# The second feed-forward product of a hybrid layer as seven block products, with weight sums made by transfers

## The chip, the cores and the metric

The kernel runs on one core of a Trainium2 chip. The metric is the device time of one execution in microseconds (us), the median of the runs shown. The engines are named as in the profile: PE (TensorE, matrix products; PEld is its loading of weights), DVE (VectorE), ACT (ScalarE), POOL (GpSimd) and SP (SyncE, which here only issues transfers). A transfer (DMA) is begun by an engine's queue and carried out by sixteen transfer engines that the whole core has. Every engine works through its own instructions in a fixed order; an instruction that waits for a semaphore holds up all that stand behind it on that engine.

## What is computed

One layer of a diffusion backbone over 512 tokens of 1024 channels: a modulated norm, two token mixers (a state-space scan and a windowed attention), their merge, a residual, a second modulated norm, a gated feed-forward network with a convolution of three taps, a residual and a last norm. The part that is changed is the last product and what follows it:

```python
def conv_ffn(h, w_up, conv_w, conv_b, w_down):
    u = dwconv_centred(h @ w_up, conv_w, conv_b)
    a, b = u[..., :D_FF], u[..., D_FF:]
    return (jax.nn.silu(a) * b) @ w_down
...
        h_lat = modulate(x, norm1_g[l], sh1, sc1)
        h_ctx = modulate(ctx, norm1_g[l], csh1, csc1)
        o_lat, o_ctx = token_mixer(h_lat, h_ctx, ...)
        x = x + gt1 * o_lat
        x = x + gt2 * conv_ffn(modulate(x, norm2_g[l], sh2, sc2), ...)
...
    return rmsnorm(x, final_g)
```

`D_FF` is 2816, so `w_down` is 2816 x 1024: 22 blocks of 128 along the summed axis, 8 blocks of 128 output channels. All data are 32-bit floats.

## The kernel before

Activations lie with channels on the 128 partitions and tokens along the free axis, so a product takes a 128 x 128 block of weights and streams 512 tokens through it. To keep the accuracy of 32-bit floats, both operands are split into a high part (a rounded copy, type fp32r) and a low part (the rest), and each product of blocks is three matrix instructions: high by high, high by low, low by high (`gemm`, L190 to L201; `half_gemm`, L1730, for 256 tokens). Weights come in pieces of up to 1024 columns. `load` (L157) issues the transfer of a piece on SP's queue into one of three raw buffers, casts the high part on ACT (L152) and subtracts on DVE for the low part (L153); high and low parts have two buffers each, so a piece can only be split when PE has read the piece before the last. `run` (L170) walks a list of steps and loads one piece ahead of the step that uses it.

The first stage (L369 to L728) is recorded through a planner, `Plan` (L282): each piece of work has an engine, a cost, needs and a rank, and the planner's order is written out on PE, ACT and DVE and kept. POOL and SP are not held to that order by the planner; their instructions stand where the program's recording layer puts them. In this stage the modulation weights (16 pieces), the tokens, the context and eight blocks of mixer weights are loaded, and the first norm is worked out: sums of squares, their mean (DVE, L570), the root on POOL (L574, once for 512 tokens and once for 256 context tokens), its spread over the partitions by PE (L256) and a copy of that on ACT (L275). With the copy, DVE scales (L526), ACT casts (L528) and DVE subtracts (L530) to make the operands `hlh`, `hll` of the tokens and `hch`, `hcl` of the context. Products of the first five of eight channel blocks run on tokens that are not yet normed and are scaled afterwards (L689); the last three need the normed ones.

Then follow attention, the state-space scan and the merge (not changed). The up stage has 22 steps (`up_step`, L1857), each with two products of 8 blocks, one for the half `a` and one for the half `b` of the feed-forward network, the convolution, the gate, and the split of the result: `up_second` (L1841) multiplies on DVE (L1847), casts on ACT (L1848) and subtracts on DVE (L1849) into `F["h"]` and `F["l"]`, 22 blocks of 512 tokens each. The down stage is seven `down_step`s (L1894) and `down_last` (L1905). A `down_step` loads one of 8 blocks of output channels in three pieces of 8, 8 and 6 blocks, sums 22 x 3 products of 512 tokens in one bank of PSUM, adds it, times the gate, to the residual `x1` (L1900) and adds its square to `q3`, for the last norm. `down_last` does the eighth block in two halves of 256 tokens, so that the norm of the first half runs beside the product of the second; behind the last product come the last add, squares, sums, the root on POOL, the spread, the scaling (L1925) and the stores.

Of the kernel before, what the change touches and what calls it, by code (L numbers as in the profile page):

```python
# [9 lines left out]
F32 = mybir.dt.float32  # L10
F32R = mybir.dt.float32r
# [28 lines left out]
def raw(ap):  # L40
    return ap.bitcast(F32)
# [3 lines left out]
def tile_hybrid_layer(  # L45
# [92 lines left out]
    for i in range(2 * NFF):  # L138
        src["up", i] = wup[i], 1024

    M_LOADS = {}

    def load_raw(key):
        a, n = src[key]
        r = wpool.tile([P, 1024], F32, tag="raw", name="wraw", bufs=3)
# [236 lines left out]
    with tc.tile_pool(name="spool", bufs=1) as sp:  # L382
# [1441 lines left out]
    def close_c1():  # L1824
        c1pool.close()
        c2pool = ctx.enter_context(tc.tile_pool(name="c2pool", bufs=1, reuse_waits="tile"))
        F["h"] = c2pool.tile([P, NFF, L], F32R, name="fh")
        F["l"] = c2pool.tile([P, NFF, L], F32R, name="fl")

# [11 lines left out]
    def up_second(a, pb, t):  # L1841
        b = tmp("tc")
        i = NFF + t
        S.activation(b, pb, AF.Identity, scale=col(V_FW, 44 + i), bias=col(V_FB, i))
        V.scalar_tensor_tensor(b[:, 1:], pb[:, :-1], col(V_FW, i), b[:, 1:], ALU.mult, ALU.add)
        V.scalar_tensor_tensor(b[:, :-1], pb[:, 1:], col(V_FW, 88 + i), b[:, :-1], ALU.mult, ALU.add)
        V.tensor_tensor(a, a, b, ALU.mult)  # L1847
        S.copy(F["h"][:, t, :], a)  # L1848
        V.tensor_tensor(F["l"][:, t, :], a, raw(F["h"][:, t, :]), ALU.subtract)  # L1849

    def far_piece():

        return tuple(F[n][:, NFF - 2 : NFF, :].rearrange("p a b -> p (a b)") for n in ("h", "l"))

    ELSEWHERE["up", 1] = far_piece

# [34 lines left out]

    q3 = hpool.tile([P, L], F32, tag="q2", name="q3")

    def down_step(o):  # L1894
        def fn(*w):
            ps = accb()
            for i, n in ((0, 8), (1, 8), (2, 6)):
                gemm([(ps, F["h"], F["l"])], w[i], nk=n, k0=8 * i, first=i == 0, last=i == 2)
            xo = x1[o // 4][:, o % 4, :]
            V.scalar_tensor_tensor(xo, ps, mod2[:, 24 + o : 25 + o], xo, ALU.mult, ALU.add)  # L1900
            add_square(q3, xo, o)

        return [("dn", 3 * o + i) for i in range(3)], fn

    def down_last(*w):  # L1905

        pf = misb()
        for u in range(2):
            half_sums(pf, q3, u)
        scaled, r = {}, {}  # L1910

        def finish(u):

            z = HALF[u]
            r3 = rms_spread(r["s"], 2)
            if u:
                r3s = tmp("tc")[:, :HL]
                S.copy(r3s, rms_spread(r["s"], 2)[:, :HL])
            for i, cs in enumerate(((0,), (1,), (4,), (2, 3), (5,), (6,), (7,)) if u else ((0, 1), (2, 3), (4, 5), (6, 7))):
                for c in cs:  # L1920
                    x = x1[c // 4][:, c % 4, z]
                    if u and c in scaled:
                        G.tensor_tensor(x, scaled[c], r3s, ALU.mult)
                    else:
                        V.scalar_tensor_tensor(x, x, col(V_FG, c), r3[:, :HL], ALU.mult, ALU.mult)  # L1925
                n, c = len(cs), cs[0]
                tc.keep_in_program_order((S if c in ((1, 2, 6) if u else (2,)) else nc.sync).dma_start(
                    out[c * P : (c + n) * P, z].rearrange("(a p) t -> p a t", a=n), x1[c // 4][:, c % 4 : c % 4 + n, z]
                ))
                yield  # L1930

        def root():
            r["s"] = half_root(pf, r["sq"], 0)

        def spread():
            r["f"] = finish(0)
            next(r["f"])
            next(r["f"])

        def add(u):  # L1940
            xo = x1[1][:, 3, HALF[u]]
            if u == 0:
                V.scalar_tensor_tensor(xo, ps[u][:, :HL], mod2[:, 31:32], xo, ALU.mult, ALU.add)
                r["sq"] = half_squares([xo])
            else:

                sq = tmp("tc")[:, :HL]
                for b in range(2):
                    z = slice(b * P, (b + 1) * P)
                    V.scalar_tensor_tensor(xo[:, z], ps[u][:, z], mod2[:, 31:32], xo[:, z], ALU.mult, ALU.add)  # L1950
                    S.activation(sq[:, z], xo[:, z], AF.Square)
                r["sq"] = [sq]

        for i, c in enumerate((4, 5)):
            scaled[c] = tmp("te")[:, :HL]
            S.activation(scaled[c], x1[1][:, c % 4, HALF[1]], AF.Copy, scale=col(V_FG, c))
        ps = [accb(), accb()]
        with tc.manual_schedule(engines={mybir.EngineType.PE}):
            for u, i in ((0, 0), (1, 0), (0, 1), (0, 2), (1, 1), (1, 2)):
                half_gemm(ps[u], F["h"], F["l"], HALF[u], w[i], (8, 8, 6)[i], 8 * i, NFF, {11: root, 17: spread} if u else {})  # L1960
                if i == 2:
                    add(u)
            next(r["f"])
            r["s"] = half_root(pf, r["sq"], 1)
            for f in (r["f"], finish(1)):
                for _ in f:
                    pass
# [27 lines left out]
def pack(  # L1995
# [45 lines left out]
    d["wdn"] = _cols(w_down, A(1024))  # L2041
# [25 lines left out]
```

## Time and profile before

| | us |
|---|---|
| median of 3 runs | 1240.38 (1240.37 to 1240.45) |
| span of the profiled execution | 1239.5 |
| PE busy | 1230.0 |
| DVE busy | 864.6 |
| ACT busy | 656.3 |
| POOL busy | 145.4 |
| first stage, to the first product behind it | about 65 |
| up stage, then down stage | to 1107.7, to 1230.0 (last product) |

The profile shows one execution, taken by the hardware profiler. Its times are microseconds from the start of the span unless marked ns. A row of the timeline gives start, duration, engine, line, operation, tiles (result before the arrow, operands behind it), shape and count, and in brackets the idle time before it and what ended it. In a group row, "x154 | 60.0, 390 | 0.0" is the count, busy time in us, mean ns of one and idle time before. Products on PE are pipelined: their durations overlap, so the distance from one start to the next is what one costs. A window row gives each engine's busy time in that stretch with the number of instructions, PE's granted clock (1.00 is full speed), the mean busy share of the sixteen transfer engines and what they moved. In the row of 40 slices a digit is the busy share of a slice in tenths.

### The profile page before, as it was taken

To read this page: it belongs to the slowest core of one execution; us is meant where nothing else is said; L and a number is where in the kernel's file an instruction comes from. 1 tells how busy PE (TensorE), PEld (TensorE's weight loads), DVE (VectorE), ACT (ScalarE), POOL (GpSimd) and SP (SyncE) were. 2 spreads that over 40 slices of the span, in tenths; PEclk is the share of its full clock that TensorE was granted. 3 is DMA by queue.
4 is the path that set the end of the run, shared out by engine and by line. 5 is a ranking of instruction groups with operands and counts; after the bars stand their busy time and mean duration, and the time that the engine had idled before them with its cause. 6 is when DMAs were issued, how large, how long until landed. Compare 5 with 4: busy or idle time off the path is not lost.

```text
span 1239.5 us, 17395 instructions
## 1 busy us (share of the span) xinstructions
PE 1230.0 (99%) x6464; PEld 1013.8 (82%) x6464; DVE 864.6 (70%) x1387; ACT 656.3 (53%) x1224; POOL 145.4 (12%) x145
## 2 busy tenths in 40 slices
PE   9999999999999999999999999999999999999997
PEld 6798888888888878777787788889888888888886
DVE  5857788888645697896987767576777767772333
ACT  5658788787454476475675653224544444442221
POOL 0000000000000052261542530000100000000000
PEclk9999999999999999999999999999999999999999
DMA  9643142222354336355365577674233333333331
GB/s 371 248 136 94 56 137 81 91 72 77 119 173 132 127 102 184 115 157 158 102 187 203 146 257 262 213 231 159 89 117 119 109 113 119 112 106 97 103 94 68
DMA packets 91189, 174.57 MB, mean 141 GB/s; under 512 B 7904, under 2 KB 43552, under 8 KB 91104
## 3 DMA queue, kind: packets, MB, share of 16 engines
q1 hardware_dynamic: 90128, 172.66, 43.9%
q8 instruction: 51, 0.84, 0.3%
q10 hardware_dynamic: 976, 0.79, 0.2%
q14 instruction: 34, 0.28, 0.1%
HBM read 150.82 MB, written 17.11 MB: 135 GB/s over the span
## 4 chain that ended last, share of the span: by engine, by line
PE 93%; DMA 3%; DVE 3%; ACT 1%; issue 0%; POOL 0%; DVEq 0%; SPq 0%; ACTq 0%; POOLq 0%
PE acc L196 21%; PE acc L199 21%; PE acc L197 21%; PE score L914 3%; PE po L963 3%; PE pt L950 2%; PE mis L536 2%; PE mis L1567 2%; PE mis L1460 2%; PE mis L1575 1%; DMA wraw<-wout 1%; PE acc L1033 1%; PE acc L1034 1%; PE acc L1035 1%; PE mis L1477 1%; PE mis L1375 1%
## 5 line engine op out<-in xcount | busy, mean ns | idle before, releaser
L153 DVE TENSOR_TENSOR wlo<-wraw,whi 128x1024 fp32r<-128x1024 f32 (+2 forms) x127 | 156.0, 1228 | 125.9 <-ACT whi L152 123.0
L152 ACT CAST whi<-wraw 128x1024 fp32r<-128x1024 f32 (+2 forms) x127 | 131.2, 1034 | 196.3 <-PE acc L197 142.5
L196 PE MATMUL acc<-hlh,whi 128*128 128x512 f32 x472 | 194.2, 411 | 0.0
L197 PE MATMUL acc<-hll,whi 128*128 128x512 f32 x472 | 185.0, 392 | 0.0
L199 PE MATMUL acc<-hlh,wlo 128*128 128x512 f32 x472 | 185.0, 392 | 0.0
L196 PE MATMUL acc<-mh,whi 128*128 128x512 f32 x368 | 143.4, 390 | 0.0
L197 PE MATMUL acc<-ml,whi 128*128 128x512 f32 x368 | 143.2, 389 | 0.0
L199 PE MATMUL acc<-mh,wlo 128*128 128x512 f32 x368 | 143.2, 389 | 0.0
L199 PEld LDWEIGHTS acc<-hlh,wlo 128*128 128x128 f32 x472 | 88.6, 188 | 19.5
L196 PEld LDWEIGHTS acc<-hlh,whi 128*128 128x128 f32 x472 | 88.8, 188 | 17.9 <-issue 3.1
L197 PEld LDWEIGHTS acc<-hll,whi 128*128 128x128 f32 x472 | 88.9, 188 | 17.4 <-issue 2.4
L1462 POOL TENSOR_TENSOR st<-st,eT 128x512 f32<-128x512 f32 x24 | 29.5, 1230 | 448.7 <-ACT st L1479 435.0
L197 PEld LDWEIGHTS acc<-ml,whi 128*128 128x128 f32 x368 | 69.1, 188 | 14.4
L196 PEld LDWEIGHTS acc<-mh,whi 128*128 128x128 f32 x368 | 69.1, 188 | 14.3
L199 PEld LDWEIGHTS acc<-mh,wlo 128*128 128x128 f32 x368 | 69.1, 188 | 14.2
L1348 DVE SCALAR_TENSOR_TENSOR ta<-acc,half,ta 128x511 f32<-128x511 f32 (+1 forms) x66 | 43.9, 665 | 27.3 <-ACT ta L1347 27.1
L923 DVE CUSTOM_DVE_ANT_0 p<-score,winm,nsink 128x512 f32<-128x512 f32 (+1 forms) x64 | 51.8, 810 | 15.3 <-PE score L914 13.8
L250 POOL TENSOR_TENSOR rs<-ms,phalf 128x2 f32<-128x2 f32 (+1 forms) x5 | 4.8, 956 | 475.2 <-DVE ms L249 475.2
L196 PE MATMUL acc<-fh,whi 128*128 128x512 f32 x154 | 60.0, 390 | 0.0
L197 PE MATMUL acc<-fl,whi 128*128 128x512 f32 x154 | 59.9, 389 | 0.0
L199 PE MATMUL acc<-fh,wlo 128*128 128x512 f32 x154 | 59.9, 389 | 0.0
L1347 ACT ACTIVATE ta<-acc,half 128x512 f32<-128x512 f32 (+1 forms) x66 | 46.9, 711 | 22.5 <-PE acc L199 21.2
(381 smaller groups left out, 2891.4 us busy)
## 6 DMA issues: line engine op xcount, KB each, us to landing
wraw<-wup SPq DMA_DIRECT2D x44, 512.0 KB, 3.4
fb<-cs_d SPq DMA_DIRECT2D x32, 512.0 KB, 6.2
wraw<-wm SPq DMA_DIRECT2D x32, 512.0 KB, 3.6
wraw<-wx SPq DMA_DIRECT2D x24, 512.0 KB, 3.6
wm<-wm SPq DMA_DIRECT2D x16, 512.0 KB, 8.4
wraw<-wz SPq DMA_DIRECT2D x16, 512.0 KB, 3.5
wraw<-wos SPq DMA_DIRECT2D x16, 512.0 KB, 4.8
wraw<-wdn SPq DMA_DIRECT2D x16, 512.0 KB, 3.5
```

The source lines that it names most:

```text
L152: S.copy(hi[:, :n], r[:, :n])
L153: V.tensor_tensor(lo[:, :n], r[:, :n], raw(hi[:, :n]), ALU.subtract)
L196: T.matmul(ps, wh, xh[:, k0 + k, :], start=a, stop=False)
L197: T.matmul(ps, wh, xl[:, k0 + k, :], start=False, stop=False)
L199: T.matmul(ps, wl, xh[:, k0 + k, :], start=False, stop=b)
L536: T.matmul(ps, w[a], h[b], start=c == 1, stop=c % n == 0, skip_group_check=True)
L914: T.matmul(ps[:, o : o + len(z) * P], Q[h][:, b * P : (b + 1) * P], k[:, j, z[0] * P : (z[-1] + 1) * P], start=v == 0 and o % 512 in (0, P ...
L923: V.tensor_tensor_reduce(p[:, :w], d["ps"][i][:, o0 : o0 + w], m, op0=ALU.add, op1=ALU.min, scale=1.0, scalar=nsink[:, h : h + 1], accum_o ...
L963: T.matmul(d["po"], vst[:, cols[x], j, :], d[y][x], start=x == 0 and y == "pth", stop=x == c - 1 and y == "ptl")
L1347: S.activation(o[:, :n], ps[:, :n], AF.Identity, scale=hcol(base_w, stride + i), bias=hcol(base_b, i))
L1348: V.scalar_tensor_tensor(o[:, 1:n], ps[:, 0 : n - 1], hcol(base_w, i), o[:, 1:n], ALU.mult, ALU.add)
L1462: G.tensor_tensor(h8(n), h8(s), bc64(eT[:, z0 : z0 + 8, c]), ALU.mult)
```

## The change

The 22 blocks of the summed axis are taken as two sets of 11 (even and odd, `DK` = 11), the 8 output blocks as two halves of 4, and the tokens as two halves of 256. A product of 2 x 2 by 2 x 2 blocks is then made with seven block products instead of eight, by sums and differences of operands before the products and of results after them. Each of the seven products `j` has 4 output blocks `q`, and each of these 11 x 3 instructions of 256 tokens.

Weights: four of the seven products take sums of weight blocks. `weight_sums` makes them in DRAM, four tensors of 4 x 704 KB, by transfers on POOL's queue: a copy, and then a transfer that adds to what lies there, in pieces of 1408 bytes. It is called behind the first stage; there are 32 such transfers. The weights of a block `q` are loaded in two pieces, of 6 and 5 blocks (`DPARTS`); from the third block on the second piece of each goes to a raw buffer of its own with five places (`dnraw`, in the room of `hlh`).

Activations: in the up stage, `f_sums` splits the first half of an even block (operand of product 0), subtracts the second half and splits that (operand of product 1), and forms with the odd block the other operands. The operands of products 2 to 6 are split in the steps of the product before them (`f_split` in `down_step`), into two buffers in turn.

Results: products 0, 2 and 4 add into two banks of PSUM and are read after each; the others have a bank each. `x_add` adds them to the residual. In `down_last`, product 6, the halves change places: the second half of the tokens is finished first.

```diff
@@ in tile_hybrid_layer, the sources of the weights
-        for u, n in ((0, 8), (1, 8), (2, 6)):
-            src["dn", 3 * i + u] = wdn[i, :, u * 1024 : u * 1024 + n * P], n * P
+    DK = NFF // 2
+    DPARTS = ((0, 6), (6, DK - 6))
+    DSUMS = {i: dpool.tile([4, P, DK * P], F32, name="dsum%d" % i) for i in (1, 2, 4, 5)}
+    for q in range(4):
+        for j, t in enumerate((wdn[0, q], DSUMS[1][q], DSUMS[2][q], wdn[1, q], DSUMS[4][q], DSUMS[5][q], wdn[3, q])):
+            for u, (k0, n) in enumerate(DPARTS):
+                src["dn", (4 * j + q) * 2 + u] = t[:, k0 * P : (k0 + n) * P], n * P
+
+    def weight_sums():
+        for j, first, more in (
+            (4, wdn[0], wdn[2]), (1, wdn[2], wdn[3]), (2, DSUMS[4], wdn[3]), (5, DSUMS[2], wdn[1]),
+        ):
+            for q in range(4):
+                G.dma_start(DSUMS[j][q], first[q])
+            for q in range(4):
+                G.dma_start(DSUMS[j][q], more[q], accum_op=ALU.add, max_dma_last_dim=DK * P)
@@ behind the first stage
         run_plan(first_.order({"PE": 5.2, "ACT": 3.0, "DVE": 3.6, "SP": 0.7}, bus=2.76))
         first.update(w=ws[1], q=B_[0, "g"], k=B_[1, "g"])
+    weight_sums()
@@ the up stage
+    def f_split(s, ks, x):
+        S.copy(F["s"][s][:, 0, ks, :], x)
+        V.tensor_tensor(F["s"][s][:, 1, ks, :], x, raw(F["s"][s][:, 0, ks, :]), ALU.subtract)
+
+    def f_sums(t):
+        p, (x, y) = t // 2, F["x"]
+        e, f, g, h = (a[:, p, z] for a in (x, y) for z in HALF)
+        one = slice(p, p + 1)
+        if t % 2 == 0:
+            f_split(0, one, x[:, one, HALF[0]])
+            V.tensor_tensor(e, e, f, ALU.subtract)
+            f_split(1, one, x[:, one, HALF[0]])
+        else:
+            V.scalar_tensor_tensor(e, e, -1.0, h, ALU.mult, ALU.subtract)
+            V.tensor_tensor(f, h, f, ALU.subtract)
+            V.scalar_tensor_tensor(F["t"][:, p, :], e, -1.0, g, ALU.mult, ALU.subtract)
-        V.tensor_tensor(a, a, b, ALU.mult)
-        S.copy(F["h"][:, t, :], a)
-        V.tensor_tensor(F["l"][:, t, :], a, raw(F["h"][:, t, :]), ALU.subtract)
+        V.tensor_tensor(F["x"][t % 2][:, t // 2, :], a, b, ALU.mult)
+        f_sums(t)
@@ the down stage
+    def product(j, q, w, ps, st, after={}):
+        s = F["s"][(0, 1, 0, 1, 0, 1, 0)[j]]
+        with tc.manual_schedule(engines={mybir.EngineType.PE}):
+            for u, (k0, n) in enumerate(DPARTS):
+                wh, wl = w[u]
+                for k in range(n):
+                    c, h, l = slice(k * P, (k + 1) * P), s[:, 0, k0 + k, :], s[:, 1, k0 + k, :]
...
+                    T.matmul(ps, wh[:, c], h, start=st and k0 + k == 0, stop=False, skip_group_check=True)
+                    T.matmul(ps, wh[:, c], l, start=False, stop=False, skip_group_check=True)
+                    T.matmul(ps, wl[:, c], h, start=False, stop=en, skip_group_check=True)
-    def down_step(o):
-        def fn(*w):
-            ps = accb()
-            for i, n in ((0, 8), (1, 8), (2, 6)):
-                gemm([(ps, F["h"], F["l"])], w[i], nk=n, k0=8 * i, first=i == 0, last=i == 2)
-            xo = x1[o // 4][:, o % 4, :]
-            V.scalar_tensor_tensor(xo, ps, mod2[:, 24 + o : 25 + o], xo, ALU.mult, ALU.add)
-            add_square(q3, xo, o)
+    def down_step(j, q):
+        def fn(*w):
...
+            chain = j in (0, 2, 4)
+            bank = F["A"][q // 2] if chain else accb()
+            ps = bank[:, q % 2 * HL : q % 2 * HL + HL] if chain else bank[:, :HL]
+            product(j, q, w, ps, j == 0 and q % 2 == 0 or not chain)
+            if 1 <= j < 6:
+                ks = slice(3 * q, min(3 * q + 3, DK))
+                f_split((j + 1) % 2, ks, OPERAND[j + 1]()[:, ks, :])
+            if chain and q % 2:
+                t = tmp("te")
+                S.copy(t, bank)
...
+            elif j == 1:
+                x_add(q, 1, 1, ps)
+                x_add(4 + q, 1, -1, ps)
...
-        + [down_step(o) for o in range(7)]
-        + [([("dn", 21 + i) for i in range(3)], down_last)],
+        + [down_step(j, q) for j in range(6) for q in range(4)]
+        + [([("dn", 48 + i) for i in range(8)], down_last)],
```

More of the change, by code (lines that the diff above doesn't have):

```diff
@@ L144, in load_raw @@
         a, n = src[key]
-        r = wpool.tile([P, 1024], F32, tag="raw", name="wraw", bufs=3)
+        if key[0] == "dn" and key[1] >= 4 and key[1] % 2:
+            if "dnraw" not in F:
+                F["dnraw"] = hpool.tile([P, 5, 6 * P], F32, tag="hlh", name="dnraw")
+            r = F["dnraw"][:, key[1] // 2 % 5, :]
+        else:
+            r = wpool.tile([P, 1024], F32, tag="raw", name="wraw", bufs=3)
         dma = nc.sync.dma_start(r[:, :n], a)
@@ L1892, in tile_hybrid_layer @@
     q3 = hpool.tile([P, L], F32, tag="q2", name="q3")
[L1894 to L1909 removed]
+    ng2 = cpool.tile([P, 4], F32, name="ng2")
@@ new lines, in tile_hybrid_layer, with x_add, half_square @@
+    OPERAND = [
+        None, None, lambda: F["x"][0][:, :, HALF[0]], lambda: F["x"][1][:, :, HALF[0]], lambda: F["x"][0][:, :, HALF[1]],
+        lambda: F["x"][1][:, :, HALF[1]], lambda: F["t"],
+    ]
+    def x_add(c, u, a, ps):
+        x = x1[c // 4][:, c % 4, HALF[u]]
+        g = ng2[:, c - 4 : c - 3] if a < 0 else mod2[:, 24 + c : 25 + c]
+        V.scalar_tensor_tensor(x, ps, g, x, ALU.mult, ALU.add)
+    def half_square(c, u):
+        x, q = x1[c // 4][:, c % 4, HALF[u]], q3[:, HALF[u]]
+        if c % 4 == 0 and (c, u) in ((0, 0), (4, 1)):
+            S.activation(q, x, AF.Square)
+        else:
+            sq = tmp("tc")[:, :HL]
+            S.activation(sq, x, AF.Square)
+            V.tensor_tensor(q, q, sq, ALU.add)
@@ L1910, in down_last @@
+    def down_last(*ws):
+        ws = [ws[2 * q : 2 * q + 2] for q in range(4)]
         scaled, r = {}, {}
@@ L1930, in finish, with sums @@
                 yield
+        pf = misb()
+        def sums(u, part, first, last):
+            rms_sums(pf[:, 2 * u : 2 * u + 2], part, 2, 0, first, last)
         def root():
-            r["s"] = half_root(pf, r["sq"], 0)
+            sums(1, q3[:, HALF[1]], True, True)
+            r["s"] = rms_root(pf[:, 2:4], 2, EPS)
         def spread():
-            r["f"] = finish(0)
+            r["f"] = finish(1)
             next(r["f"])
             next(r["f"])
[L1940 to L1957, printed above, removed]
-        with tc.manual_schedule(engines={mybir.EngineType.PE}):
[L1959 to L1967, printed above, removed]
+        def early():
+            sums(0, q3[:, HALF[0]], False, False)
+            for _ in r["f"]:
+                pass
```

60 lines of the change are left out of this document (52 added, 8 removed).

## The prediction

> **What bounds the kernel now.** I read the page first (busy shares, the 40 slices), then the windows of the first 50 us, then the timelines of POOL, DVE and ACT there, last the groups and the timeline of the stage that is rewritten.
>
> ```profile
> span 1239.5 us, 17395 instructions
> PE 1230.0 (99%) x6464; PEld 1013.8 (82%) x6464; DVE 864.6 (70%) x1387; ACT 656.3 (53%) x1224; POOL 145.4 (12%) x145
> ...
> DMA  9643142222354336355365577674233333333331
> ```
>
> TensorE (PE) is busy 99% of the span, so the time is PE's work plus whatever makes PE wait. An instruction saved on PE is worth its interval; a wait added anywhere in PE's order is paid in full. The transfer engines are less than half busy in nearly all slices, except the first (31 us each).
>
> ```profile
> core 0: us, PE busy (x) PEld busy (x) DVE busy (x) ACT busy (x) POOL busy (x), PEclk, DMA share, GB/s
> 0.00:10.00 10.00, 8.85 (x60) 7.10 (x64) 2.23 (x12) 3.37 (x6) 0.78 (x9) 1.00 0.80 283
> 10.00:20.00 10.00, 10.00 (x78) 6.62 (x78) 6.40 (x15) 5.49 (x10) 0.00 (x0) 1.00 1.04 410
> 20.00:30.00 10.00, 10.00 (x79) 6.85 (x78) 6.84 (x14) 6.44 (x13) 0.00 (x0) 1.00 1.03 414
> 30.00:40.00 10.00, 10.00 (x78) 6.76 (x76) 6.16 (x16) 5.08 (x13) 1.01 (x1) 1.00 1.03 410
> 40.00:50.00 10.00, 10.00 (x66) 7.85 (x63) 9.56 (x19) 6.58 (x13) 0.70 (x1) 1.00 0.55 195
> ```
>
> From 10 to 40 us the sixteen transfer engines are full (share 1.03) at about 412 GB/s: the start-up is limited by its loads, 15.2 MB in the first 40 us, some 16 MB in the burst, 39 us of full-rate transfer. POOL does almost nothing then, but that little is on PE's path:
>
> ```profile
> 1.21 0.10 POOL L396 MEMSET rmsc<- 128x1 f32 x1
> 35.31 1.01 POOL L574 TENSOR_TENSOR rs<-ms,phalf 128x4 f32<-128x4 f32 x1 [34.00 <-DVE ms L570]
> 43.02 0.70 POOL L574 TENSOR_TENSOR rs<-ms,phalf 128x2 f32<-128x2 f32 x1 [6.70 <-DVE ms L570]
> 425.76 1.07 POOL L1462 TENSOR_TENSOR st<-st,eT 128x512 f32<-128x512 f32 x1 [382.04 <-ACT st L1479]
> ```
>
> These are the two roots of the first norm (tokens at 35.31, context at 43.02), each begun as soon as its mean is there. After them POOL is free until 425.76. What hangs on the second:
>
> ```profile
> 42.79 0.15 DVE L570 TENSOR_SCALAR ms<-acc 128x2 f32<-128x2 f32 x1
> ...
> 44.98 0.38 PE L256 MATMUL acc<-ident,rs 128*128 128x128 f32 x2
> ...
> 45.39 0.37 ACT L275 COPY r_c<-acc 128x256 f32<-128x256 f32 x1 [3.17 <-PE acc L256]
> 45.66 1.34 ACT L528 ACTIVATE hlh<-xsb,s 128x512 fp32r<-128x512 f32 x2
> ```
>
> PE and ACT run this stage in a fixed order. PE's spread at 44.98 and ACT's copy at 45.39 take the context root; behind the copy stand the casts of token operands (45.66) that PE multiplies next. A late context root therefore stops all three engines, although context itself is first multiplied some 20 us later.
>
> **The change, part by part.**
>
> *The adding transfers (the large term).* In the built order of the changed kernel POOL's queue reads: memsets; 4 copies DRAM to DRAM; 4 adding transfers, each waiting for its copy; 4 copies; 4 adding ones; 1 copy; the token root; 3 copies; 1 adding transfer, which waits for the first adding transfer of the second group and the first copy of the third; and only then the context root. Nothing holds back the first four, so they start at 1.2 us, into the full engines. Nine copies and eight adding transfers (the rest of the second group stands ahead of the third group's copy in the same queue) must be through before the context root, each of 128 x 11 x 128 floats = 704 KB.
>
> No transfer of POOL and no adding one is in this trace. The nearest prices:
>
> ```profile
> wraw<-wup SPq DMA_DIRECT2D x44, 512.0 KB, 3.4
> fb<-cs_d SPq DMA_DIRECT2D x32, 512.0 KB, 6.2
> ...
> q<-tc SPq DMA_DIRECT2D x16, 128.0 KB, 2.3
> ```
>
> A copy at the full rate: 0.721 MB / 412 GB/s = 1.75 us. An adding transfer at least the same; at most at the rate of the smallest pieces here, fb in 512-byte pieces, 704/512 x 6.2 = 8.5 us. I take twice the copy, 3.5 us, since it reads two operands, nearer to the lower row because its pieces (1408 bytes) are larger than fb's. Ahead of the context root: 9 x 1.75 + 8 x 3.5 = 44 us (30 us by the low price, 84 by the high). Full engines share these with 39 us of loads, of which the order needs nearly all by then; whoever goes first, the sum is the same: 1.2 + 39 + 44 + 2 us for a completion (the small q row) = 86 us. The mean waited from 42.94; so the root, and PE with it, is 43 us late. By the low price 1.2 + 39 + 30 + 2 = 72, 29 us late; by the high one 126, 83 us late. The token root stands behind 9 copies and 4 adding transfers, needs most of the loads as well, and comes earlier: within this term, not beside it.
>
> The Trainium skill, "DMA: Bandwidth & Descriptors", section "Issuing engines are not separate DMA queues", says transfers begun by different engines end on the same 16 transfer engines and interleave. This trace, with one busy queue, does not show it. By that rule the term is the 43 us; if POOL's queue had capacity of its own, it would be the chain alone, 1.2 + 44 + 2 = 47 us, 4 us late.
>
> *The rest of these transfers* (7 copies, 8 adding ones: 7 x 1.75 + 8 x 3.5 = 40 us) runs on into the attention part, where the engines were half full (0.55 in the last window above). Loads there are issued well ahead, but the small rearrangements (q<-tc, 2.3 us) are not, and they would share the engines: I take 3 us, from 0 to 10. They end near 150 us, far ahead of POOL's next work at 425.76 and of the use of the sums at 1107.
>
> *The up stage.* Per pair of its 22 steps the two 512-wide high/low pairs go; in come 2 casts (ACT) and 6 operations (DVE), 256 wide. On DVE:
>
> ```profile
> L1849 DVE TENSOR_TENSOR fl<-ta,fh 128x512 fp32r<-128x512 f32 x18 | 12.5, 693 | 12.4 <-ACT fh L1848 12.4
> ...
> L1925 DVE SCALAR_TENSOR_TENSOR x<-x,vec,mis 128x256 f32<-128x256 f32 x14 | 5.8, 474 | 2.9 <-PE mis L256 2.9
> ...
> 930.00:1000.00 70.00, 70.00 (x312) 57.95 (x312) 49.31 (x64) 30.43 (x39) 0.00 (x0) 1.00 0.35 113
> 1106.00:1212.00 106.00, 106.00 (x471) 87.77 (x470) 35.48 (x39) 26.61 (x32) 0.00 (x0) 1.00 0.32 95
> ```
>
> 3 x 0.47 for 0.69, 0.7 us more per 10.9 us step, with DVE at 49 of 70 us: hidden under PE's 48 products, cost 0; without that cover it would be 22 x 0.7 = 16 us, of which I allow 3.
>
> *The products.* Now 462 of 512 tokens, then 132 of 256:
>
> ```profile
> 1107.69 0.49 PE L196 MATMUL acc<-fh,whi 128*128 128x512 f32 x1
> ...
> 1212.32 0.39 PE L199 MATMUL acc<-fh,wlo 128*128 128x512 f32 x1
> ...
> 1212.55 0.28 PE L1736 MATMUL acc<-fh,whi 128*128 128x256 f32 x1
> ...
> 1215.30 0.28 PE L1738 MATMUL acc<-fh,wlo 128*128 128x256 f32 x1
> ...
> 1229.98 0.28 PE L1738 MATMUL acc<-fh,wlo 128*128 128x256 f32 x1
> ```
>
> Intervals: (1212.32 - 1107.69) / 461 = 0.227 us; (1215.30 - 1212.55) / 23 = 0.120 us, more than half of 0.227. Before: 462 x 0.227 + 132 x 0.120 = 120.7. After: 7 x 4 x 33 = 924 x 0.120 = 110.9. Seven for eight would be 15 us; at half width 9.8 us are left.
>
> *What feeds them.* The weights' high/low split grows from 176 to 308 blocks in less time, and pieces are 6 and 5 blocks (2.16 and 1.80 us of PE) in two buffers each.
>
> ```profile
> L153 DVE TENSOR_TENSOR wlo<-wraw,whi 128x768 fp32r<-128x768 f32 x8 | 7.7, 958 | 26.9 <-ACT whi L152 26.9
> L152 ACT CAST whi<-wraw 128x768 fp32r<-128x768 f32 x8 | 6.7, 837 | 28.2 <-PE acc L197 16.0 <-issue 6.9 <-PE acc L1737 5.3
> ...
> L1943 DVE SCALAR_TENSOR_TENSOR x<-acc,mod,x 128x256 f32<-128x256 f32 x1 | 0.5, 484 | 3.3 <-PE acc L1738 3.3
> ...
> 32.74 0.82 DVE L512 TENSOR_TENSOR w0l<-w,w0h 128x640 fp32r<-128x640 f32 x1 [1.07 <-ACT w0h L502]
> 39.00 0.73 ACT L502 CAST w0h<-w 128x640 fp32r<-128x640 f32 x1 [0.57 <-PE mis L536]
> ```
>
> A 6-block piece: cast 0.84 and subtraction 0.96, with some 0.3 us to the cast behind PE's last reader (a 256-wide product is out 0.28 us after its start) and an estimated 0.2 back to PE: 2.3 us, against 1.80 + 0.24 + 0.12 = 2.16 until its low part is read. So there is no slack even with both engines idle: up to 0.1 us per step. DVE's sum per product of 15.84 us: 4 x (0.96 + 0.82) + operand subtractions 3 x 0.96 + 0.69 + eight adds x 0.48 = 14.6 us; in the fifth product, with squares, about 16. And the built order puts two or three 768-wide operand subtractions between two weight subtractions just after the start of five products: some 1 us each, over 2 in the sixth. Sum of stalls: 28 x 0.05 + 6 = 7 us (from 0 to 14). The stage: -9.8 + 7 = -3 (from -10 to +4). Its loads grow to 28 x 704 KB, 178 GB/s, hidden as the raw pieces have three and five buffers and a load takes 3.5 us. The tail behind the last product (1229.98) keeps its steps; only the halves change places.
>
> **Sum.** 1239.5 + 43 + 3 + 0 - 3 = 1282.5; outside the span lie 1240.4 - 1239.5 = 0.9, so about 1283 us against the runs' 1240.38.
>
> **Rivals.**
> 1. *The price of an adding transfer is wrong.* Same mechanism, other size: 29 us late, no other loss, 1239.5 + 29 - 10 + 0.9 = 1259; at the high price, 83 us late, with the other upper ends 1239.5 + 83 + 10 + 3 + 4 + 0.9 = 1340. For it: no such row exists. Against the high end: fb's pieces are a third as long.
> 2. *Not slower.* The seventeen transfers run on capacity that the loads leave, and an adding one costs a copy's price: the chain ends at 1.2 + 30 + 2 = 33 us, before the context mean at 42.9, and the roots are on time; only the last stage counts, 1240.4 - 3 = 1237. It decides from 42 us down. For it: 412 GB/s are reads of SBUF loads, a transfer within DRAM does not write SBUF. Against: the engines themselves show a share of 1.03.
> 3. *POOL itself is slow to issue* (writing out the pieces of each adding transfer): the roots wait for POOL's issuing even where the engines have room. At 12 us each, 8 x 12 + 9 + 3 = 108 us, 65 late: 1239.5 + 65 + 0.9 - 3 = 1302. No row speaks for it or against it.
> 4. *The last stage becomes DVE's.* At its upper end it loses 4 us instead of winning 3: 1290 with the rest as forecast.
>
> **How the numbers follow.** Forecast as summed, give or take 10: 0.45; rival 1 low 0.2, high 0.1; rival 3 0.1; rival 4 0.1; rival 2 0.05. The range from 1256 to 1332 takes in the low price, the slow issue and most of the way to the high price. Faster by more than 0.2% (2.5 us, about what a measurement of this kernel can tell from no change) is rival 2: 0.05. Within it: rival 2 with a worse last stage, 0.01. Slower: 0.94.
>
> **What would show it.** Right: POOL's two roots at about 60 and 86 us instead of 35 and 43, their idle time ended by transfers or queue, PE idle before the context spread, full engines until about 85 us; then PE as dense as before, 256-wide products 0.120 us apart with gaps of about 1 us at the starts of products. Wrong: the context root near 43 us, or a start-up lengthened with POOL's roots on time; or gaps all through the last stage.

## The result, and the profile after

The changed kernel takes 1308.24 us (median of 4 runs, 1307.86 to 1308.5), the kernel before 1240.41 us beside it: a ratio of 1.0545 (95% interval 1.0531 to 1.056). The prediction said slower, 1283 us with a range from 1256 to 1332. The direction is right, the time lies inside the range and 25 us beyond the forecast.

The page of the changed kernel: span, busy shares, and the slices (32.7 us each).

```profile
span 1306.1 us, 18420 instructions
PE 1248.7 (96%) x6790; PEld 1037.5 (79%) x6790; DVE 924.3 (71%) x1518; ACT 686.8 (53%) x1289; POOL 169.1 (13%) x177
PE   6667999999999999999999999999999999999997
...
DMA  9999831432224723644635657777323333336553
```

PE has holes in the first four slices (and, as before, in the last), and the transfer engines are full in these four. The windows of that part (columns as in the prediction: busy time and count of each engine, granted clock, share of the transfer engines, GB/s):

```profile
0.00:50.00 50.00, 30.12 (x165) 19.67 (x165) 10.74 (x27) 10.47 (x18) 10.44 (x23) 0.77 1.04 314
50.00:100.00 50.00, 33.83 (x171) 22.33 (x171) 17.40 (x38) 12.80 (x29) 10.73 (x13) 0.74 1.06 299
100.00:150.00 50.00, 39.31 (x159) 32.05 (x160) 27.26 (x50) 23.92 (x41) 6.11 (x8) 0.78 1.08 268
```

The engines stay full (1.04 to 1.08) until nearly 150 us, not until about 85 as forecast. PE runs out of work, and its granted clock is 0.74 to 0.78 there, 1.00 in the kernel before. From 150 us on PE is full again (50.00 of the next 50 us, at 1.00, the transfer engines at 0.41). POOL's timeline shows the roots (start, duration, instruction, and in brackets the idle time before it and what ended it):

```profile
47.61 1.04 POOL L154 DMA_DIRECT2D dsum<-wdn  x1 [30.18 <-DMA dsum<-wdn]
...
75.08 1.04 POOL L594 TENSOR_TENSOR rs<-ms,phalf 128x4 f32<-128x4 f32 x1 [19.18 <-DVE ms L590]
76.09 1.56 POOL L152 DMA_DIRECT2D dsum<-dsum  x3
88.73 1.07 POOL L154 DMA_DIRECT2D dsum<-wdn  x1 [11.09 <-DMA dsum<-dsum]
89.42 1.12 POOL L594 TENSOR_TENSOR rs<-ms,phalf 128x2 f32<-128x2 f32 x1
...
498.30 1.06 POOL L1483 TENSOR_TENSOR st<-st,eT 128x512 f32<-128x512 f32 x1 [367.75 <-ACT st L1500]
```

The context root comes at 89.42 instead of 43.02 us, 46.4 us late. Which share of this is the loads' and which the queue's, DVE's timeline says: the mean that the root takes was ready at 84.28 us, against 42.94 before.

```profile
84.13 0.15 DVE L590 TENSOR_SCALAR ms<-acc 128x2 f32<-128x2 f32 x1
```

So 41.3 us of the 46.4 passed before the mean was there, with the engines full, and for 5.1 us the root then stood in POOL's queue behind a transfer that waited for another to land. But POOL's next work on data, at 425.76 before, is now at 498.30, 72.5 us late. Another 26 us go after the root. ACT's timeline shows where it waits:

```profile
97.79 1.04 ACT L624 CAST whi<-wraw 128x1024 fp32r<-128x1024 f32 x1 [13.97 <-DMA wraw<-wq]
98.74 0.37 ACT L295 COPY r_c<-acc 128x256 f32<-128x256 f32 x1
...
117.20 0.69 ACT L618 ACTIVATE tb<-mis,gb 128x512 f32<-128x512 f32 x1 [5.59 <-DMA ts_d<-tb]
...
129.18 0.69 ACT L618 ACTIVATE tb<-mis,gb 128x512 f32<-128x512 f32 x1 [7.11 <-DMA ts_d<-tb]
```

The copy of the context root, at 45.39 before, is 53.3 us late: a cast that waits for a load of wq stands ahead of it in ACT's order, and adds 7 us to the root's 46. Later the gates (L618) wait for stores of tb to leave their buffers, 5.59 and 7.11 us, and the casts of context queue behind them. What PE loses by it, its own waits from 89 to 150 us say, the longest first:

```profile
PE acc L216 <- ACT hch L548: 8.4, 1, 8.4
PE acc L556 <- ACT whi L624: 6.6, 1, 6.6
```

The first is the wait for the cast of context, the second the one for the cast of wq. With three shorter ones PE's waits there come to 18.3 us, none of which the kernel before has from 42 to 90 us. The other 8 of the 26 us are not waits: PE works slowly. Its granted clock was 0.50 from 95.1 to 105.3 and from 125.8 to 142.8 us, and there two products of 512 tokens are 0.43 us apart instead of 0.227:

```profile
139.33 0.63 PE L216 MATMUL acc<-hlh,whi 128*128 128x512 f32 x1
139.76 0.63 PE L217 MATMUL acc<-hll,whi 128*128 128x512 f32 x1
```

Both stretches began while PE was waiting, so part of the work behind a wait ran at half speed as well. The last stage, from its first to its last product, in PE's timeline:

```profile
1179.40 0.36 PE L1960 MATMUL mis<-fs,whi 128*128 128x256 f32 x1
...
1296.60 0.28 PE L1962 MATMUL acc<-fs,wlo 128*128 128x256 f32 x1
```

That is 117.2 us, against 1229.98 - 1107.69 = 122.3 before: a gain of 5.1 us. Together: 46.4 + 26.1 - 5.1 = 67.4 us, and the medians differ by 67.8.

### The profile page after: what moved, and what is told of

Its sections match the earlier page's. It is cut to its first block, busy times and chain, and to the rows that moved or that the text cites. A ratio compares the mean times of both kernels' runs of the same rounds, so it can differ in the third digit from the quotient of the medians.

```text
span 1306.1 us, 18420 instructions
## 1 busy us (share of the span) xinstructions
PE 1248.7 (96%) x6790; PEld 1037.5 (79%) x6790; DVE 924.3 (71%) x1518; ACT 686.8 (53%) x1289; POOL 169.1 (13%) x177
## 4 chain that ended last, share of the span: by engine, by line
PE 89%; DMA 9%; ACT 1%; DVE 1%; issue 0%; SPq 0%; POOL 0%; DVEq 0%; ACTq 0%; POOLq 0%
PE acc L216 19%; PE acc L219 19%; PE acc L217 19%; PE score L935 3%; PE po L984 3%; DMA xsb<-xT 2%; PE pt L971 2%; PE mis L1588 2%; DMA wraw<-wq 2%; DMA wm<-wm 2%; PE mis L1481 2%; PE acc L1962 2%; PE acc L1960 2%; PE acc L1961 2%; DMA ts_d<-tb 1%; PE mis L1596 1%
## 5 line engine op out<-in xcount | busy, mean ns | idle before, releaser
L216 PE MATMUL acc<-hch,whi 128*128 128x256 f32 x176 | 55.6, 316 | 8.4 <-ACT hch L548 8.4
L951 ACT ACTIVATE p<-p,mneg 128x512 f32<-128x512 f32 (+1 forms) x64 | 49.7, 777 | 15.4 <-DVE mneg L944 14.8
L979 DVE TENSOR_TENSOR ptl<-pt,pth 128x512 fp32r<-128x512 f32 x72 | 47.5, 686 | 8.6 <-ACT pth L975 7.7
```

Source lines behind the costliest of these rows:

```text
L216: T.matmul(ps, wh, xh[:, k0 + k, :], start=a, stop=False)
L951: S.activation(p, p, AF.Exp, bias=d["mneg"][:, i : i + 1], scale=-1.0, accum_out=d["den"][:, i : i + 1])
L979: V.tensor_tensor(d["ptl"][x], d["pt"][x], raw(d["pth"][x]), ALU.subtract)
```

## The experiments

Each was timed beside the kernel before (1240.2 to 1240.4 us). Two theories stood against each other: *engine time* (the transfers take the sixteen engines from the loads and stores, wherever they run) and *order* (POOL's queue holds the roots, and all the rest follows from that).

### The transfers left out

```diff
-        for j, t in enumerate((wdn[0, q], DSUMS[1][q], DSUMS[2][q], wdn[1, q], DSUMS[4][q], DSUMS[5][q], wdn[3, q])):
+        for j, t in enumerate((wdn[0, q], wdn[2, q], wdn[3, q], wdn[1, q], wdn[2, q], wdn[1, q], wdn[3, q])):
...
-    weight_sums()
```

> The changed kernel without its 32 transfers: products 1, 2, 4 and 5 of the last stage read plain weight blocks where the changed kernel reads sums, so the sums of weight blocks are left out of what is computed. Theory 1 (the whole loss is made by the transfers, in the first 150 us; the last stage wins 5 us): first root near 35 us, second near 43 us as in the kernel before, first down product at about 1108, last stage 117 us, time 1240.4 - 5 = 1235 us. Rival (part of the 72 us comes from other edits, the new operand splits of the up stage or the different order of the program): above 1240 us, with the first down product later than 1112.

Measured: 1235.93 us (ratio 0.9965, 0.9954 to 0.9977), with the context root at 43.09 us and the first product of the last stage at 1106.89 us (1107.69 before). This kernel leaves the sums of weights out of what is computed. All of the loss is the transfers'; the other edits gain 4.5 us.

### The transfers behind the roots

```diff
-                G.dma_start(DSUMS[j][q], first[q])
+                tc.keep_in_program_order(G.dma_start(DSUMS[j][q], first[q]))
...
-                G.dma_start(DSUMS[j][q], more[q], accum_op=ALU.add, max_dma_last_dim=DK * P)
+                tc.keep_in_program_order(G.dma_start(DSUMS[j][q], more[q], accum_op=ALU.add, max_dma_last_dim=DK * P))
```

> All 32 transfers are kept, but are issued by POOL behind both roots, so that nothing of POOL's queue is held and they begin at about 43 us. Theory 1 (the transfers take engine time from the loads; 97 us of it in all): the roots are on time at 35 and 43 us, the burst is undisturbed, but the 97 us of transfers now meet the loads and stores of attention, at a DMA share that was 0.3 to 0.55 there; some of the 26 us that were lost behind the second root stay, and the time is 1245 to 1265 us. Theory 2 (the loss is the place of the roots behind the transfers in POOL's queue, and all that follows from it): about 1236 us.

Measured: 1257.04 us (1.0131, 1.0116 to 1.0147), with the context root at 42.76 us. The windows of this kernel:

```profile
50.00:100.00 50.00, 45.83 (x246) 40.89 (x246) 28.46 (x50) 24.36 (x43) 12.16 (x16) 0.93 1.07 262
100.00:150.00 50.00, 40.34 (x194) 33.59 (x193) 27.01 (x56) 28.57 (x59) 10.20 (x12) 0.86 1.09 295
```

With the root on time, 1257.0 - 1235.9 = 21 us are still lost, because the same transfers fill the engines (1.07 to 1.09) from 50 to 150 us. Order alone would have given 1236. Attention does not carry 32 unpaced transfers for 3 us. Here too the granted clock is below 1.00 (0.93 and 0.86).

### The transfers alone, in the kernel before

The 32 transfers were added to the kernel before, at the place they have in the changed one; nothing reads them.

```diff
+    def weight_sums():
+        wd = [wd4[i // 2, i % 2] for i in range(4)]
+        for j, first, more in (
+            (4, wd[0], wd[2]), (1, wd[2], wd[3]), (2, DSUMS[4], wd[3]), (5, DSUMS[2], wd[1]),
+        ):
+            for q in range(4):
+                G.dma_start(DSUMS[j][q], first[q])
+            for q in range(4):
+                G.dma_start(DSUMS[j][q], more[q], accum_op=ALU.add, max_dma_last_dim=DK * P)
...
+    weight_sums()
```

> The kernel before with the 32 transfers added at the start, in the changed kernel's order; nothing reads their results, the last stage has its eight products. Theory 1 (the transfers alone make the loss, the last stage gives 5 us back): first down product about 72 us later than before, time 1240.4 + 72 = 1312 us. Rival (the loss needs the changed stages too): under 1300 us.

Measured: 1308.38 us (1.0548, 1.0531 to 1.0564), 4 under the expectation; the context root came at 92.48 us. The transfers make the loss without any other edit. Here the mean was ready at 78.21 us, so POOL's queue held the root for 14 us, against 5 in the changed kernel: order has a part in the late root, the smaller one in both.

### Only the eleven transfers behind the root held back

```diff
+    for _ in range(21):
+        SUMS.pop(0)()
...
+                while SUMS and a["engine"] == "ACT" and a["start"] >= -86.0 + 6.0 * (32 - len(SUMS)):
+                    next_sum()
```

SUMS lists the 32 transfers in their order; next_sum issues the next one and lets it wait for ACT's last instruction so far.

> The changed kernel with the 21 transfers that stand ahead of the context root in POOL's queue left at the start, and the other 11 let go only from about 200 us on, one every 6 us. The root is therefore as late as in the changed kernel (89 us against 43). Theory 1 (26 us of the loss come from the transfers that still run behind the root, most of all from the eleven issued there): the 46 us of the late root stay, of the 26 us only what the last four of the 21 still cost, about 5: 1237 + 51 = 1288 us. Theory 2 (a late root is enough: the loads of attention have bunched up behind it, and the 26 us come with it): 1305 us.

Measured: 1292.92 us (1.0422, 1.0407 to 1.0438), with the context root at 89.11 us, as late as in the changed kernel. Its window from 100 us on:

```profile
100.00:150.00 50.00, 48.57 (x271) 43.78 (x271) 31.53 (x57) 27.08 (x50) 0.00 (x0) 0.97 0.53 162
```

The root is as late, but from 100 to 150 us the engines are half free and PE is busy 48.6 of 50 us instead of 39.3. So 1308.2 - 1292.9 = 15.3 of the 26 us belong to the eleven transfers issued behind the root. Some 11 us beyond the root's 46 stay (expected: 5). Four transfers issued just before the root still run then, and PE's granted clock was 0.50 from 89.2 to 102.8 us; what each of these costs was not separated.

### Eight plain copies: do the queues share the engines?

```diff
+        for j, first in ((4, wd[0]), (1, wd[2])):
+            for q in range(4):
+                G.dma_start(DSUMS[j][q], first[q])
```

> The kernel before with 8 plain copies of 704 KB (DRAM to DRAM) issued by POOL at the start, nothing reads them, and nothing in POOL's queue waits for them: the roots stand behind 8 issues of about 1 us. Theory 1 (POOL's transfers and SP's loads share the same 16 engines): 8 copies at 1.75 us (bytes at the full rate) to 2.4 us (as measured where copies ran alone in the paced kernel) delay the loads by 14 to 19 us; both roots move by that, and the time is 1254 to 1260 us. Theory 2 (the loss of the changed kernel comes from the order of POOL's queue; the engines have room for transfers within DRAM): roots at 35 and 43 us, 1240 us.

Measured: 1255.53 us (1.0123, 1.0108 to 1.0138). POOL's timeline:

```profile
1.38 4.33 POOL L149 DMA_DIRECT2D dsum<-wdn  x8
49.78 1.04 POOL L584 TENSOR_TENSOR rs<-ms,phalf 128x4 f32<-128x4 f32 x1 [44.07 <-DVE ms L580]
```

POOL is free from 5.7 us on and waits for the mean; no order holds anything. Yet the token root is 14.5 us late (and the context root, at 57.49, as much), which is 8 x 1.75 = 14.0 with the copy's price by bytes. The loads and the copies share one capacity. This is what the rule that the prediction weighed (the Trainium skill, "DMA: Bandwidth & Descriptors", section "Issuing engines are not separate DMA queues") says, and it ends rival 2.

### Plain copies instead of adding ones, in large and in small pieces

First all 32 transfers as plain copies, in packets of 5.6 KB and, for eight of them, 45 KB (the sizes in the trace):

```diff
-                G.dma_start(DSUMS[j][q], more[q], accum_op=ALU.add, max_dma_last_dim=DK * P)
+                G.dma_start(DSUMS[j][q], more[q])
```

> The kernel before with 32 transfers at the start in the changed kernel's order and with the same waits, but all 32 are plain copies; nothing reads them. Theory 1 (an adding transfer takes twice a copy's engine time: 2 us and 4 us under full engines, together 97 us): 32 x 2 = 64 us instead of 97, the loss of 68 us with the adding ones shrinks to 45, 1285 us. Theory 2 (an adding transfer is no dearer than a copy, bytes decide): 1308 us as with the adding ones. Theory 3 (the chains of waits decide, not engine time): little changed, above 1300 us.

Then the same copies, cut smaller. The limit of 1408 was meant to give pieces of 1408 bytes, as the adding ones have. In the trace the adding transfers do have packets of 1408 bytes, but these copies have 5120 packets of 4224 bytes and 512 of 2816; the expectation below is wrong in this, and in the 22.5 KB that it gives the largest packets of the first run.

```diff
-                G.dma_start(DSUMS[j][q], first[q])
+                G.dma_start(DSUMS[j][q], first[q], max_dma_last_dim=1408)
...
-                G.dma_start(DSUMS[j][q], more[q])
+                G.dma_start(DSUMS[j][q], more[q], max_dma_last_dim=1408)
```

> As the kernel before with 32 plain copies, but every copy is cut into pieces of 1408 bytes, the size that the adding transfers have (instead of 5.6 to 22.5 KB). Nothing reads the copies. In the kernel with large pieces POOL's queue took 63 to 82 per cent of the engines between 77 and 110 us, and SP's loads and stores took 23 to 26 us to land. Theory 1 (the engines take turns between the two queues piece by piece, so large pieces starve SP): SP's share rises, its transfers land in under 15 us, the stall of 21 us on a store goes, and the time falls below 1301, to 1280 to 1295. Theory 2 (small pieces are what made the adding transfers slow, adding itself costs nothing): the copies now take as long as adding ones, the context root moves from 77 to 92 us, and the time is about 1308. Theory 3 (size of pieces plays no part): 1301.

Measured: 1301.09 us (1.0482, 1.0464 to 1.0499) in large pieces, 1290.85 us (1.0411, 1.0395 to 1.0427) in smaller ones. The queues over the whole span (packets, MB, share of sixteen engines; q0 is POOL's), of the kernel before with adding transfers, with copies, and with smaller copies:

```profile
q0 software_dynamic: 9856, 23.07, 7.5%
```

```profile
q0 software_dynamic: 3712, 23.07, 4.6%
```

```profile
q0 software_dynamic: 6144, 23.07, 4.7%
```

Times the spans (1304.3, 1299.1, 1289.1 us) that is 98, 60 and 61 us of engine time. A copy costs 60/32 = 1.9 us in either size of packet; an adding transfer (98 - 16 x 1.9)/16 = 4.2 us, more than twice as much. A plain copy in packets of 1408 bytes was not run. That such packets alone explain the price is unlikely, for the trace has 133 ns on average for a packet of 1408 bytes of an adding transfer and 120 ns for one of 2816 bytes of a smaller copy.

But the large copies lose 61 us with 60 us of engine time, where theory 1 expected 45; 1301 us is what theory 3 (the chains of waits decide) allowed for. The smaller copies have the same waits and lose 51 us, so the waits alone do not decide either. Their context root came at 73.55 us, that of the large ones at 77.18, 34 late; the rest is lost behind it. The queues in the window from 77 to 90 us, large packets first, smaller ones second, each with the landing time of SP's stores in its last row:

```profile
q0 software_dynamic: 573, 3.41, 70.7%
q1 hardware_dynamic: 602, 1.01, 21.3%
ts_d<-tb SPq DMA_DIRECT2D x2, 256.0 KB, 23.9
```

```profile
q0 software_dynamic: 814, 3.06, 66.7%
q1 hardware_dynamic: 811, 1.44, 31.6%
ts_d<-tb SPq DMA_DIRECT2D x2, 256.0 KB, 15.3
```

In this window both queues move about the same number of packets, 573 against 602 and 814 against 811, as if the engines took turns packet by packet, and POOL's large packets carry 3.4 times SP's bytes. In the next 20 us the counts are 690 against 662 with large packets, but 1501 against 893 with smaller ones; whether SP's queue had a backlog all through that time, the profile does not say. A store of 256 KB, 2.2 us in the kernel before, lands after 24 us, and ACT stands for it. ACT's timeline, large and smaller packets:

```profile
111.49 0.69 ACT L612 ACTIVATE tb<-mis,gb 128x512 f32<-128x512 f32 x1 [20.78 <-DMA ts_d<-tb]
```

```profile
99.85 0.69 ACT L612 ACTIVATE tb<-mis,gb 128x512 f32<-128x512 f32 x1 [12.00 <-DMA ts_d<-tb]
```

The Trainium skill, "DMA: Bandwidth & Descriptors", section "Queues, rings and completion order", has this rule: an engine goes round its queues one packet at a time. The packet counts from 77 to 90 us agree. Of what the expectation for the smaller copies named, the time came (1280 to 1295); SP's transfers landed after 15.3 to 16.8 us, not under 15, and the wait of 21 us fell to 12 and did not go.

### The transfers paced through attention

```diff
+    def next_sum():
+        act = next(i for i in reversed(nc.cur_bb.bb.instructions) if i.engine == mybir.EngineType.Activation)
+        dma = tc.keep_in_program_order(SUMS.pop(0)())
+        tc.add_manual_dep(
+            dma.ins, act.name,
+            mybir.DependencyInfo(mybir.DependencyClass.Sync, mybir.DependencyReason.DATA), reason="next_sum",
+        )
...
+                while SUMS and a["engine"] == "ACT" and a["start"] >= 20.0 + 6.0 * (32 - len(SUMS)):
+                    next_sum()
```

> The changed kernel with its 32 transfers behind the roots and spread out over attention: one is let go about every 6 us, each waiting for an instruction of ACT, from some 50 to 270 us. Theory 1 (engine time is what counts: 3.0 us of 16 engines per transfer in every 6 us, half of the engines, beside a share of 0.3 to 0.55 of other transfers): the engines suffice, roots at 35 and 43 us, time 1235 to 1240 us, at or under the kernel before. Rival (each adding transfer delays the small stores and loads around it, whatever the mean share): 1245 us or more, with ACT and PE waiting for transfers all over the first 270 us.

Measured: 1236.87 us (0.9968, 0.9958 to 0.9979), and the second time, beside the last experiment:

> The paced kernel a second time, beside its variant: 1236.9 us, 0.3 per cent under the kernel before, with the upper end of the interval below 1.

1236.12 us (0.9968, 0.9956 to 0.9981). The windows of the first of these:

```profile
100.00:150.00 50.00, 50.00 (x296) 43.65 (x295) 41.50 (x90) 41.64 (x83) 4.34 (x6) 1.00 0.60 158
150.00:200.00 50.00, 50.00 (x269) 42.66 (x268) 41.80 (x84) 41.99 (x79) 6.10 (x8) 1.00 0.91 219
200.00:300.00 100.00, 99.97 (x555) 85.73 (x554) 84.13 (x182) 78.92 (x155) 13.34 (x17) 1.00 0.82 203
```

The same 32 transfers, one about every 6 us from 115 to about 300 us, raise the share of the engines to 0.60 to 0.91, and PE is busy throughout. Against the kernel without the sums (1235.93) they cost at most 1 us, although their engine time is longer here, 9.3% of 1233.6 = 115 us against 7.4% of 1306.1 = 97 us in the changed kernel. It beats both kernels.

### Two tries at the last stage

On the paced kernel, the operand subtractions were first moved from DVE to POOL, then cut, with their casts, into single blocks:

```diff
-        V.tensor_tensor(F["s"][s][:, 1, ks, :], x, raw(F["s"][s][:, 0, ks, :]), ALU.subtract)
+        (G if ks.stop - ks.start > 1 else V).tensor_tensor(F["s"][s][:, 1, ks, :], x, raw(F["s"][s][:, 0, ks, :]), ALU.subtract)
```

> The paced kernel with the 128x768 and 128x512 operand subtractions of the last stage moved from DVE to POOL, which is idle there. Theory 1 (the stage's remaining stalls come from DVE's operand subtractions between two weight subtractions): two to three microseconds less, 1234 to 1235 us against 1236.9. Theory 2 (the stalls come from ACT's casts or from the operands being late, or POOL's slower subtraction makes them late): 1237 us or more.

```diff
-                f_split((j + 1) % 2, ks, OPERAND[j + 1]()[:, ks, :])
+                for k in range(ks.start, ks.stop):
+                    f_split((j + 1) % 2, slice(k, k + 1), OPERAND[j + 1]()[:, slice(k, k + 1), :])
```

> The paced kernel with the operand casts and subtractions of the last stage cut into single blocks (256 wide instead of 512 to 768), so that the scheduler can put them between the weight subtractions. Theory 1 (whole 768-wide operand subtractions in DVE's and ACT's queues make the gaps of about 1 us at the starts of products): one to three microseconds less than the paced kernel. Theory 2 (the gaps come from the buffers, which are free only when the product before has ended): no change beyond 1 us; the fixed cost of 66 more instructions could make it slower.

Measured: 1255.72 us (1.0123, 1.0108 to 1.0138) with POOL, a clear miss, and 1234.24 us (0.9952, 0.994 to 0.9965) with single blocks, the best of all. DVE's weight subtractions of the last stage, in the paced kernel and in the one with POOL (busy time, mean ns of one):

```profile
L181 DVE TENSOR_TENSOR wlo<-wraw,whi 128x768 fp32r<-128x768 f32 x28 | 26.8, 957 | 16.3 <-ACT whi L180 16.2
```

```profile
L181 DVE TENSOR_TENSOR wlo<-wraw,whi 128x768 fp32r<-128x768 f32 x28 | 32.9, 1174 | 26.2 <-ACT whi L180 26.1
```

These are averages over instructions with and without POOL at work. One of POOL's stretches, with DVE's instructions before and in it, shows the two apart:

```profile
1181.43 8.18 POOL L1864 TENSOR_TENSOR fs<-fx,fs 128x768 fp32r<-128x768 f32 x4 [12.67 <-ACT fs L1863]
1180.70 0.42 DVE L1960 TENSOR_TENSOR q<-q,tc 128x256 f32<-128x256 f32 x1
1182.33 1.76 DVE L181 TENSOR_TENSOR wlo<-wraw,whi 128x768 fp32r<-128x768 f32 x1 [1.21 <-ACT whi L180]
1184.02 0.47 DVE L1951 SCALAR_TENSOR_TENSOR x<-acc,mod,x 128x256 f32<-128x256 f32 x1
...
1186.41 2.06 DVE L1960 TENSOR_TENSOR q<-q,tc 128x256 f32<-128x256 f32 x1
```

An addition with both operands in SBUF takes 0.42 us alone and 2.06 beside POOL, a weight subtraction 1.76 against 0.96 on average in the paced kernel; the addition that reads one operand from PSUM stays at 0.47. PE pays in waits for the weights' low parts:

```profile
PE acc L1972 <- DVE wlo L181: 8.5, 5, 3.3
```

With four more such waits (3.5 us) and one of 4.1 us for a cast that makes 16.1 of the 19 us, and none of PE's waits there is for the operands that POOL makes. The single blocks take away waits of PE for the weight casts: the group of the paced kernel, then of this one (us in total, times, longest):

```profile
PE acc L1970 <- ACT whi L180: 2.0, 3, 0.9
```

```profile
PE acc L1970 <- ACT whi L180: 0.9, 1, 0.9
```

From its first to its last product the stage takes 116.1 instead of 117.2 us; the medians (1236.12 and 1234.24, timed together) differ by 1.9.

## Why the prediction was right, and where it was not

*The adding transfers ahead of the root* (43 us, root at 86): right. The root came at 89.42, 46.4 us late. The prices were near too: 1.9 and 4.2 us measured for 1.75 and 3.5 taken. The mechanism, shared engines, is shown by the eight plain copies, and in the changed kernel 41.3 of the 46.4 us passed before the mean was ready; the place in the queue added 5.1. The token root was forecast at about 60 and came at 75.08; it waited 19.18 us for DVE's mean, so for loads, not for the queue.

*"The rest of these transfers"* (3 us, from 0 to 10): this is the step that failed, and most of the 25 us that the forecast is short. Its amount of transfer time was nearly right, its price in waiting was not: some 26 us passed behind the root, of which holding back eleven transfers gave back 15, and 21 us were lost even with the root on time. The step argued that engines with a share of 0.55 have room and that loads are issued well ahead. (Nor do the slices say that the engines are less than half busy in nearly all: 13 of the 40 digits are 5 or more.) Room on average is not enough: while POOL has a backlog, its queue takes a large share of the engines, about every other packet where it was counted, and the few transfers that PE's and ACT's order waits for (a load of wq, the stores of tb) take several times as long. A second term the step left out: some 8 of the 26 us are no waits but PE working slowly, at a granted clock of 0.50 behind them. The paced kernel is the counter-proof: the room is there, if the transfers come one at a time.

*The up stage* (0, at most 3): right. The kernel without the sums has every other edit, its last stage begins at 1106.89 us against 1107.69, and it is 4.5 us under the kernel before, as the gain of the last stage asks.

*The products and what feeds them* (-3, from -10 to +4): right within its bounds, at -5.1. The before side was taken as 120.7, without the steps between products that its own timeline holds (122.3). The after side came out, 110.9 + 7 = 117.9 against 117.2, but the 7 us were meant as stalls, and PE's waits are only 2.6 us: three for ACT's casts (2.0 together) and one for DVE's subtractions (0.6), not five of DVE's. The rest of the 6.3 us beyond 110.9 are distances of more than 0.120 us around waits and the steps between products, which the sum left out on this side too; so that the sum came so near is in part luck.

*The rivals.* Price wrong: no, as above. Own capacity: no, by the eight copies. POOL slow to issue: an adding transfer's issue takes 1.0 us, where the rival assumed 12, and POOL's idle time ends with transfers landing (30.18 and 11.09 us), so no. The last stage DVE's: not in this kernel, but the try with POOL shows how near it is: over a fifth more on DVE's weight subtractions, with the longer additions, went with a loss of 19 us, most of it in PE's waits for these subtractions.

## What to carry to other kernels

Price a background transfer by its engine time and by what is in flight beside it: a backlog on a second queue can take half of the packets or more, and the small stores and loads in the compute order wait several times longer, even where the average share looks half free. Let such transfers go one at a time through the part with room, behind the start-up burst: the same 32 transfers then cost at most 1 us instead of 72. Look at PE's granted clock behind its waits: here part of the next work ran at half speed. Before moving work to an idle engine, look for what it shares with the busy one.

## What the runs showed of the hardware

- A transfer within DRAM that adds cost 4.2 us of the sixteen engines for 704 KB, a plain copy 1.9 us, in the kernel before with such transfers at its start; copies in packets of 4.2 KB and of 5.6 to 45 KB cost the same. The price is not fixed: the same 32 transfers took 97 us in the changed kernel and 115 us paced.
- Two queues that both wait for the engines moved equal numbers of packets in one window (814 against 811, and 573 against 602 with larger packets in POOL's queue), so the size of its packets decides a queue's share of the bytes there.
- PE's granted clock was 1.00 or 0.50 in stretches. At 0.50 products of 512 tokens were 0.43 us apart, at 1.00 0.227; the two stretches at 0.50 behind the context root of the changed kernel began while PE was waiting.
- POOL's subtractions, which read SBUF, slowed DVE's instructions with two SBUF operands (0.42 to 2.06 us for a 128x256 addition), and not the addition with one operand in PSUM (0.47 us beside POOL). The Trainium skill, "SBUF — State Buffer", section "Who interferes with whom", says that a DVE instruction with two SBUF inputs contends with a GpSimd one that reads SBUF; these rows agree.
